# Regrouping the FFN chunks of a fp32 decoder: groups of three, a down projection by seven products in four parts, and a first group that adds into seeded banks

## Chip, cores and metric

The kernel runs on one core of a Trainium2 chip. The metric is device time in microseconds (us) of one execution. TensorE is called PE (its weight loads PEld), VectorE DVE, ScalarE ACT, GpSimd POOL, SyncE SP.

## The reference

A trunk of two layers over one sequence of 512 tokens with 1024 features (DEPTH 2, D_FF 2816), all in fp32. Each layer is an FFN at half weight, a mixer, and a second FFN at half weight; the mixer of layer 0 is a gated linear attention (GLA), that of layer 1 a stick-breaking attention (SB). A last RMSNorm follows.

```python
def swiglu(h, w_gate, w_up, w_down):
    return (jax.nn.silu(h @ w_gate) * (h @ w_up)) @ w_down
...
# Layer i: x += 0.5*FFN_a(RMSNorm(x)); x += Mixer(RMSNorm(x)); x += 0.5*FFN_b(RMSNorm(x))
```

The work thus runs FFN 1, GLA, FFN 2, FFN 3, SB, FFN 4, final norm.

## The kernel before

**fp32 from parts.** Each fp32 operand is cut into a high part (a cast to fp32r, by ScalarE: `wh` for weights, L534; `hh`, `nh`, `th` for activations, L1231) and the remainder (a subtraction on VectorE: `wl`, L535; `hl`, `nl`, `tl`, L1232). A product is three matmuls: high x high, low x high, high x low (`mm3`, L477). Weights are raw tiles (`raw` of 8x256 per partition, two buffers; `rawd` for the down projection, two buffers) loaded by SP (L500) and cut once, into pools of four wide tiles (`wh`, `wl`) or one small tile ("few").

**x** lies transposed in SBUF as eight tiles of 128 features x 512 tokens (`xs[0]` to `xs[7]`). PSUM has eight banks, handed out by tag (`ps_f`, `ps_d`, `ps_w`, `ps_z`, `ps_q` name the accumulators in the profile).

**An FFN** takes its 2816 features as 11 chunks of 256. For each chunk gate and up are formed, multiplied, cut (`close`, `close_first`, `close_second`), and later multiplied by the chunk's rows of `w_down`. Chunks are put into groups (L1042): while one group's gate and up are computed, the down products of the group before stand between them. Gate and up go in two ways: by direct products for the first two chunks, and by *seven products* for the other nine (`seven`, L1110): a 2x2 block product (features by halves of the tokens, 256 columns) of seven block products instead of eight, at the price of sums of weight blocks on VectorE (L1119 to L1126) and of copies between banks.

**The down projection** has the same two ways.

- *Direct* (`down`, L740 to L773): a bank `ps_d` of 128 x 512 sums over the group's features for one tile of x; when it is complete, VectorE adds half of it to x (L767).
- *Seven products* (`seven_down`, L775 to L872), for groups of two chunks that DOWN_SEVEN names. It runs in two parts of 256 columns of each half of `w_down`, so that one part serves x tiles m = 0, 1 of the part in both halves of the model (xs[k] and xs[k+4]). VectorE forms four sums of weight blocks (L796, L797, L803, L804). Then seven products of 2 chunks each (matmul L812) go, for each m, into three banks: w takes b11, is copied to z by ScalarE (L830), and then takes t2, t3 and t4, one after the other; after each of them VectorE adds the bank to a quarter of two x tiles (L818), and the next product adds onto the same bank. q takes t1 and b22, z takes b21. For t3 ScalarE copies the bank to `u3` first (L857). A product on a bank must wait until the bank's value before has been read.

In the last FFN the last group is written by tokens (`back_tok`).

**The order of the work.** Entries of a feed list say in which order weights are loaded and cut (`Entry.split`, L519; `Feed.ready`, L555 cuts for up to three entries ahead). Over this stands a `Planner`: it takes all recorded instructions, prices each (`price`, L171), plans each engine's order by these prices and due times, and pins that order. So a changed price moves instructions in every stage. At a stage's end the function `nxt` of the last group prepares the next one: ScalarE and VectorE form squares (L913, L914) and the cut of the scaled x (`xh` L924, `xl` L925) as each x tile is complete.

```python
        GROUPS = ((0, 2), (2, 4), (4, 6), (6, 7), (7, 9), (9, 11))
        DOWN_SEVEN = (1, 2, 4)
```

With these numbers six of 11 chunks (groups 1, 2 and 4) go down by seven products, the other five directly.

Of the kernel before, what the change touches and what calls it, by code (L numbers as in the profile page):

```python
# [48 lines left out]
class Planner:  # L49
# [31 lines left out]
    def gather(self):  # L81
# [11 lines left out]
        for i in self.bb.instructions:  # L93
# [7 lines left out]
            sizes, psum_in, wide = [], False, 0  # L101
            for write, refs in ((False, i.ins), (True, i.outs)):
                for r in refs:
# [3 lines left out]
                    ap = [(int(s), int(n)) for s, n in b.ap]  # L107
                    n = 1
# [50 lines left out]
            self.cost[k], self.step[k] = self.price(i, kind, e, sizes, psum_in)  # L159
# [11 lines left out]
    def price(self, i, kind, e, sizes, psum_in):  # L171
        n = max((s[1] for s in sizes), default=1)
        if e == "PE":
            types = [s[2] for s in sizes]
            if any("bfloat16" in t for t in types):
                return 270.0, max(64.0, 0.43 * n)
            if any("float32r" in t for t in types):
                return 165.0 + 0.42 * n, max(112.0, 0.422 * n)
            moving = sizes[0][1]
            full = sizes[1][1] == P and not kind.endswith("Transpose") and not getattr(i, "is_transpose", False)  # L180
            return 150.0 + 0.9 * n, max(58.0, 0.845 * moving) * (2 if full and moving in (1, P) else 1)
# [260 lines left out]
def decoder(ctx: ExitStack, tc: tile.TileContext, a: dict, out: bass.AP):  # L442
# [31 lines left out]
    def mm(ps, l, r, first, last):  # L474
        nc.tensor.matmul(ps, l, r, start=first, stop=last)  # L475

    def mm3(ps, wh, wl, mh, ml, first, last):  # L477
        mm(ps, wh, turns(mh), first, False)
        mm(ps, wl, turns(mh), False, False)
        mm(ps, wh, turns(ml), False, last)  # L480
# [5 lines left out]
    class Chunk:  # L486
# [51 lines left out]
    class Feed:  # L538
# [15 lines left out]
        def ready(self, i, gone):  # L554

            used = -gone
            for e in self.q[i : i + 3]:
                n = sum(n * m >= 1024 for _, _, n, m in e.units)
# [181 lines left out]
    def down(w, r0, nf, hs, part, nxt, late=0):  # L740
# [7 lines left out]
        def body(W):  # L748
# [3 lines left out]
            def prod(m, fs):  # L752
                if m == len(acc):
                    acc.append(psum("ps_d"))
                s = slice(m * P, (m + 1) * P)
                for f in fs:
                    mm3(acc[m], wh[:, f, s], wl[:, f, s], hs[f][0], hs[f][1], f == 0, f == nf - 1)
# [4 lines left out]
            for m in range(nd):  # L762
# [4 lines left out]
                nc.vector.scalar_tensor_tensor(  # L767
                    out=x, in0=flat(ps), scalar=0.5, in1=x, op0=ALU.mult, op1=ALU.add
                )
# [6 lines left out]
    def seven_down(pool, w, r0, hs, part):  # L776
# [16 lines left out]
        def sums_12(_):  # L793
            a11, _, a21, a22 = halves()
            s = v["s12"] = pool().tile([P, 4, 256], F32, tag="s", bufs=4, name="s12")
            nc.vector.tensor_tensor(out=s[:, 0:2], in0=a21, in1=a22, op=ALU.add)  # L796
            nc.vector.tensor_tensor(out=s[:, 2:4], in0=s[:, 0:2], in1=a11, op=ALU.subtract)  # L797
            return s

        def sums_34(_):  # L800
            a11, a12, a21, _ = halves()
            s = pool().tile([P, 4, 256], F32, tag="s", bufs=4, name="s34")
            nc.vector.tensor_tensor(out=s[:, 0:2], in0=a11, in1=a21, op=ALU.subtract)  # L803
            nc.vector.tensor_tensor(out=s[:, 2:4], in0=a12, in1=v["s12"][:, 2:4], op=ALU.subtract)  # L804
            return s

        def prod(ps, w, k0, m, b, first):
            for c in range(2):
                bh, bl = (turns(t) for t in hs[c][b])
                wh, wl = (t[:, k0 + c, m * P : (m + 1) * P] for t in w)  # L810
                for n, (l_, r_) in enumerate(((wh, bh), (wl, bh), (wh, bl))):
                    st["pe"] = nc.tensor.matmul(  # L812
                        ps, l_, r_, start=first and c + n == 0, stop=c == 1 and n == 2, skip_group_check=True
                    ).ins

        def add(m, up, col, ps):
            x = pair(xs[part * 2 + m + 4 * up][:, col * H : col * H + H])
            nc.vector.scalar_tensor_tensor(out=x, in0=ps, scalar=0.5, in1=x, op0=ALU.mult, op1=ALU.add)  # L818

        def body_1(W):  # L820
            a11, s, v["a2"] = W
            ws, zs, qs = [], [], []
            for m in range(2):
                ws.append(psum("ps_w")[:, 0:H])
                prod(ws[m], a11, 0, m, "b11", True)
            for m in range(2):
# [7 lines left out]
            for m in range(2):  # L834
                qs.append(ps[:, m * H : (m + 1) * H])
                prod(qs[m], s, 0, m, "t1", m == 0)
            for m in range(2):
                add(m, 1, 1, flat(qs[m]))
            yield
            for m in range(2):  # L840
                prod(ws[m], s, 2, m, "t2", False)
                add(m, 0, 1, flat(ws[m]))
            yield
            for m in range(2):
# [5 lines left out]
        def body_2(W):  # L850
            (s,) = W
            ws, qs = v["w"], v["q"]

            u3 = pool().tile([P, 2, H], F32, tag="c", bufs=1, name="u3")
            for m in range(2):
                prod(ws[m], s, 0, m, "t3", False)
                nc.scalar.copy(pair(u3[:, m]), flat(ws[m]))  # L857
                add(m, 1, 1, pair(u3[:, m]))
            yield
            for m in range(2):  # L860
                prod(qs[m], s, 2, m, "b22", False)
            for m in range(2):
                add(m, 0, 1, flat(qs[m]))
            yield
            for m in range(2):
                prod(ws[m], v["a2"], 2, m, "t4", False)
# [3 lines left out]
        units = [(lower, lambda t: halves()[0], 2, 256), (lower, sums_12, 4, 256), (lower, lambda t: halves()[1::2], 4, 256)]  # L870
        feed.q.append(Entry(units, body_1))
        feed.q.append(Entry([(lower, sums_34, 4, 256)], body_2))  # L872
# [162 lines left out]
    class FFN:  # L1035
# [6 lines left out]
        GROUPS = ((0, 2), (2, 4), (4, 6), (6, 7), (7, 9), (9, 11))  # L1042
        NORMED, SEVEN, AHEAD = 6, 2, 2
        DOWN_SEVEN = (1, 2, 4)
        SEVEN_UP = (2, 3, 4, 5, 6, 7, 8, 9, 10)

        def __init__(self, wg, wu, wd, gi, nxt, first=False, last=False):
            self.gi, self.normed = gi, False
            self.after_ffn = bool(phases) and isinstance(phases[-1], FFN)
            self.defer, self.gates = [], []  # L1050
# [4 lines left out]
            for group, (c0, c1) in enumerate(self.GROUPS):  # L1055
                slots, put = 2 * (c1 - c0), 0
                if group == 1:

                    for put in range(self.AHEAD):
                        down(*downs[put], late=put == 0)  # L1060
                    put = self.AHEAD
                for i in range(slots):
                    c, f = c0 + i // 2, i % 2
                    if f == 0:
# [17 lines left out]
                    if group - 1 in self.DOWN_SEVEN and f == 0 and c == c0:  # L1082
                        args = (lambda: self.tp, wd, self.GROUPS[group - 1][0] * 256, self.hs[group - 1])
                        seven_down(*args, 0)
                        seven_down(*args, 1)
# [5 lines left out]
                    while c >= self.SEVEN and put < len(downs) * (i + 1) // slots:  # L1091
# [6 lines left out]
                downs = [(wd, c0 * 256, n, self.hs[group], part, nxt if end else None) for part in range(n)]  # L1098
                if group in self.DOWN_SEVEN:
                    downs = []  # L1100
            self.count = len(feed.q) - base
# [182 lines left out]
        def close(self, t, group):  # L1284
            h = self.hp.tile([P, T], F32R, tag="hh", name="hh")
# [10 lines left out]
        def close_second(self, o0, o1, group):  # L1296
# [19 lines left out]
            if len(self.hs[group]) == 1:  # L1316
                for i in (2, 3):
                    h, l = (t[:, H:T] for t in self.n[i])
                    b[f"t{i + 1}"] = self.cut(h, l, ts[:, i])
            else:  # L1320

                h = sp.tile([P, T], F32R, tag="sq", name="t34")
                l = sp.tile([P, T], F32R, tag="ss", name="t34")
                self.cut(h, l, ts[:, 2:4].rearrange("p a b -> p (a b)"))
                b["t3"], b["t4"] = (h[:, 0:H], l[:, 0:H]), (h[:, H:T], l[:, H:T])

        def run(self, between=None):
            with tc.tile_pool(name="hp", bufs=8, reuse_waits="tile") as self.hp, tc.tile_pool(
                name="tp", bufs=5, reuse_waits="tile"
# [997 lines left out]
```

## Time and profile before

| | us |
|---|---|
| median of 3 runs (lowest, highest) | 1750.26 (1749.68, 1750.9) |
| the profiled execution, its own time | 1753.55 |
| its span, first to last instruction | 1751.6 |
| PE busy in the span | 1741.9 |
| DVE busy | 1586.3 |
| ACT busy | 1078.2 |
| FFN 1, 22.7 to 332.0: PE busy, DVE busy | 308.88, 300.73 |
| GLA, 343.0 to 547.0 | 203.99, 164.90 |
| FFN 2, 547.0 to 869.0 | 321.55, 308.79 |
| FFN 3, 869.0 to 1188.0 | 318.93, 304.42 |
| SB, 1188.0 to 1422.0 | 232.97, 179.67 |
| FFN 4, 1422.0 to 1720.0 | 298.00, 287.87 |

The span runs from the first to the last instruction; the rest of the execution's own time lies around it. "PE ps_q <- DVE x" in the list of waits is PE idle ahead of a matmul into ps_q that a VectorE write to x released. In a group's row, the figures behind the first bar are busy us and mean ns of one, behind the second the idle time of the engine just before them. In a timeline a row shows start, duration, engine, line, operation and the tiles (output <- inputs). A matmul's duration is longer than the step to the next, since they are pipelined. The window rows give, for each engine, busy us and instructions, then the granted clock of TensorE, the DMA engines' share and GB/s.

### The profile page before, as it was taken

How to read it: one execution, taken by the hardware profiler on the slowest of the kernel's cores; microseconds unless marked ns; L12 is line 12 of the kernel's file. 1: busy time of each engine (PE TensorE's matmuls, PEld its weight loads, DVE VectorE, ACT ScalarE, POOL GpSimd, SP SyncE). 2: the span in 40 equal slices, each digit the busy share in tenths (PEclk: the TensorE clock that was granted, in tenths of full speed). 3: DMA queues.
4: the chain of work that ended last, by engine and by line, in shares of the span. 5: the costliest groups of instructions: out<-in, count | busy, mean ns of one | idle time of the engine just before them, and what ended most of it. 6: DMA issues, size and time to landing. Idle time of an engine off the chain costs nothing.

```text
span 1751.6 us, 31640 instructions
## 1 busy us (share of the span) xinstructions
PE 1741.9 (99%) x12810; PEld 1630.5 (93%) x12810; DVE 1586.3 (91%) x2688; ACT 1078.2 (62%) x1898; POOL 9.9 (1%) x24
## 2 busy tenths in 40 slices
PE   9999999999999999999999999999999999999998
PEld 8999999888888999999989999999888889999997
DVE  8999999787888989999899999996898679999996
ACT  7556566554656565565655566566888755665655
POOL 0000000100000000000000000000000000000000
PEclk9999999999999999999999999999999999999999
DMA  6333333321223333333323333332222233333422
GB/s 190 125 98 120 97 122 121 106 70 53 73 97 97 121 116 102 97 121 113 126 77 119 99 107 121 109 103 79 61 73 73 73 97 121 121 97 104 130 93 73
DMA packets 176710, 179.27 MB, mean 102 GB/s; under 512 B 4082, under 2 KB 166180, under 8 KB 176564
## 3 DMA queue, kind: packets, MB, share of 16 engines
q1 hardware_dynamic: 175712, 175.91, 32.1%
q8 instruction: 100, 1.64, 0.4%
q0 software_dynamic: 608, 1.05, 0.2%
q14 instruction: 46, 0.38, 0.1%
q10 hardware_dynamic: 244, 0.29, 0.0%
HBM read 175.17 MB, written 2.10 MB: 101 GB/s over the span
## 4 chain that ended last, share of the span: by engine, by line
PE 85%; DVE 11%; ACT 1%; issue 1%; DMA 1%; DVEq 0%
PE ps_w L1134 18%; PE ps_f L475 17%; PE ps_d L475 10%; PE ps_q L1134 9%; PE ps_w L812 5%; PE ps_t L475 5%; PE ps_b L475 5%; PE ps_z L1134 5%; DVE wl L535 4%; PE ps_q L812 3%; DVE x L818 1%; PE ps_z L812 1%; PE ps_z L1815 1%; DMA rawd<-in_ffn_w_down_dram 1%; PE ps_S L475 1%
## 5 line engine op out<-in xcount | busy, mean ns | idle before, releaser
L535 DVE TENSOR_TENSOR wl<-raw,wh 128x1024 fp32r<-128x1024 f32 x241 | 256.5, 1066 | 42.0 <-ACT wh L534 41.4
L534 ACT CAST wh<-s 128x1024 fp32r<-128x1024 f32 x192 | 201.7, 1051 | 148.1 <-DVE s L1126 41.5
L534 ACT CAST wh<-raw 128x1024 fp32r<-128x1024 f32 x241 | 221.6, 921 | 78.6 <-PE ps_f L475 33.6
L1134 PE MATMUL ps_w<-th,wh 128*128 128x256 f32 x864 | 238.2, 276 | 0.2
L1134 PE MATMUL ps_w<-tl,wh 128*128 128x256 f32 x864 | 237.7, 275 | 0.0
L1134 PE MATMUL ps_w<-th,wl 128*128 128x256 f32 x864 | 237.7, 275 | 0.0
L535 DVE TENSOR_TENSOR wl<-s,wh 128x1024 fp32r<-128x1024 f32 x192 | 235.2, 1226 | 2.7 <-ACT wh L534 2.6
L475 PE MATMUL ps_f<-xh,wh 128*128 128x512 f32 x432 | 166.8, 386 | 0.0
L1134 PEld LDWEIGHTS ps_w<-th,wh 128*128 128x128 f32 x864 | 166.0, 192 | 0.7 <-ACT o L1167 0.7
L1134 PEld LDWEIGHTS ps_w<-tl,wh 128*128 128x128 f32 x864 | 166.0, 192 | 0.0
L1134 PEld LDWEIGHTS ps_w<-th,wl 128*128 128x128 f32 x864 | 166.0, 192 | 0.0
L475 PE MATMUL ps_f<-xl,wh 128*128 128x512 f32 x432 | 163.8, 379 | 0.0
L475 PE MATMUL ps_f<-xh,wl 128*128 128x512 f32 x432 | 163.8, 379 | 0.0
L475 PE MATMUL ps_d<-hh,wh 128*128 128x512 f32 x288 | 109.4, 380 | 0.0
L475 PE MATMUL ps_d<-hl,wh 128*128 128x512 f32 x288 | 109.3, 380 | 0.0
L475 PE MATMUL ps_d<-hh,wl 128*128 128x512 f32 x288 | 109.2, 379 | 0.0
L535 DVE TENSOR_TENSOR wl<-rawd,wh 128x512 fp32r<-128x512 f32 (+1 forms) x108 | 93.0, 867 | 1.4 <-ACT wh L534 1.4
L534 ACT CAST wh<-rawd 128x512 fp32r<-128x512 f32 (+1 forms) x108 | 80.6, 764 | 21.0 <-PE ps_d L475 12.0
L475 PEld LDWEIGHTS ps_f<-xl,wh 128*128 128x128 f32 x432 | 81.7, 189 | 11.5
L475 PEld LDWEIGHTS ps_f<-xh,wh 128*128 128x128 f32 x432 | 81.8, 189 | 11.0
L475 PEld LDWEIGHTS ps_f<-xh,wl 128*128 128x128 f32 x432 | 81.8, 189 | 10.7
L1134 PE MATMUL ps_q<-th,wh 128*128 128x256 f32 x288 | 79.3, 275 | 0.0
(349 smaller groups left out, 5506.1 us busy)
## 6 DMA issues: line engine op xcount, KB each, us to landing
raw<-in_ffn_w_gate_dram SPq DMA_DIRECT2D x43, 1024.0 KB, 5.4
raw<-in_ffn_w_up_dram SPq DMA_DIRECT2D x43, 1024.0 KB, 5.3
rawd<-in_ffn_w_down_dram SPq DMA_DIRECT2D x84, 512.0 KB, 3.5
raw<-in_gla_w_in_dram SPq DMA_DIRECT2D x12, 1024.0 KB, 5.2
raw<-in_sb_w_in_dram SPq DMA_DIRECT2D x16, 512.0 KB, 3.8
raw<-in_gla_w_out_dram SPq DMA_DIRECT2D x4, 1024.0 KB, 5.0
raw<-in_sb_w_in_dram SPq DMA_DIRECT2D x4, 1024.0 KB, 5.1
raw<-in_sb_w_out_dram SPq DMA_DIRECT2D x4, 1024.0 KB, 5.1
```

The source lines that it names most:

```text
L475: nc.tensor.matmul(ps, l, r, start=first, stop=last)
L534: nc.scalar.copy(h[:, k], part)
L535: nc.vector.tensor_tensor(out=l[:, k], in0=part, in1=h[:, k].bitcast(F32), op=ALU.subtract)
L812: st["pe"] = nc.tensor.matmul(ps, l_, r_, start=first and c + n == 0, stop=c == 1 and n == 2, skip_group_check=True).ins
L818: nc.vector.scalar_tensor_tensor(out=x, in0=ps, scalar=0.5, in1=x, op0=ALU.mult, op1=ALU.add)
L1134: st["pe"] = nc.tensor.matmul(o, l_, r_, start=first and j + n == 0, stop=j == 3 and n == 2, skip_group_check=True).ins
L1815: nc.tensor.matmul(o_, l_, r_, start=first, stop=last, skip_group_check=True)
```

## The change

1. **Groups.** Chunks are grouped 1, 3, 3, 3, 1 (last FFN: 1, 3, 3, 2, 2). Groups 1, 2 and 3 go down by seven products: nine chunks in FFN 1 to 3, eight in the last.
2. **Seven-product down in four parts.** With n chunks in a group a part takes 128 columns per half and one m (`per` = 1): each product is 3 chunks, 9 matmuls of 256 columns. The loads become 128x6x128 (384 KB). Sums and cuts become 384 and 768 columns. The last part of group 3 is held until just ahead of the last group's direct downs. Groups of two chunks keep `per` = 2.
3. **Seeded banks.** For the first group (one chunk), ScalarE writes 2x into the `ps_d` bank first (L761 of the changed kernel), the products accumulate onto it, and ScalarE writes the bank times 0.5 back to x (L777), in place of VectorE's add. In FFN 1 this holds for x tiles 2 to 7, in the others for all eight.
4. **Pools.** `rawd` has three buffers instead of two, the pool of temporaries four instead of five; a tile counts as small ("few") up to 512 columns, not below 1024. The cuts of t3 and t4 are joined, and lie in other tiles.
5. **Planner's prices.** Transposes, full fp32 matmuls and scans are priced differently.

The core of the diff:

```diff
-        GROUPS = ((0, 2), (2, 4), (4, 6), (6, 7), (7, 9), (9, 11))
+        GROUPS = ((0, 1), (1, 4), (4, 7), (7, 10), (10, 11))
+        LAST_GROUPS = ((0, 1), (1, 4), (4, 7), (7, 9), (9, 11))
+        SEEDED = (0,)
-        DOWN_SEVEN = (1, 2, 4)
+        DOWN_SEVEN = (1, 2, 3)
...
             def prod(m, fs):
                 if m == len(acc):
                     acc.append(psum("ps_d"))
+                    if part * nd + m >= seeds:
+                        x = pair(xs[part * nd + m])
+                        nc.scalar.activation(flat(acc[m]), x, AF.Copy, scale=2.0)
...
-                nc.vector.scalar_tensor_tensor(
-                    out=x, in0=flat(ps), scalar=0.5, in1=x, op0=ALU.mult, op1=ALU.add
-                )
+                if k >= seeds:
+                    nc.scalar.activation(x, flat(ps), AF.Copy, scale=0.5)
+                else:
+                    nc.vector.scalar_tensor_tensor(
+                        out=x, in0=flat(ps), scalar=0.5, in1=x, op0=ALU.mult, op1=ALU.add
+                    )
...
-    def seven_down(pool, w, r0, hs, part):
+    def seven_down(pool, w, r0, hs, part, n, per):
+        W_ = per * P
         lower, upper = (
-            Chunk(w[r0 : r0 + 4 * P, c : c + 256].rearrange("(f p) c -> p f c", p=P), 4, 256)
-            for c in (part * 256, 512 + part * 256)
+            Chunk(w[r0 : r0 + 2 * n * P, c : c + W_].rearrange("(f p) c -> p f c", p=P), 2 * n, W_)
+            for c in (part * W_, 512 + part * W_)
         )
...
-            for c in range(2):
+            for c in range(n):
...
-            for m in range(2):
+            for m in range(per):
                 ws.append(psum("ps_w")[:, 0:H])
...
+                        b0, b1 = self.GROUPS[group - 1]
+                        per = 2 if b1 - b0 == 2 else 1
+                        parts = [(*args, part, b1 - b0, per) for part in range(4 // per)]
+                        if group + 1 == len(self.GROUPS) and not last:
+                            held = parts.pop()
+                        for x in parts:
+                            seven_down(*x)
...
-                    self.t = st["few"].tile([P, self.n, self.m], F32, tag="rawd", bufs=2, name="rawd")
+                    self.t = st["few"].tile([P, self.n, self.m], F32, tag="rawd", bufs=3, name="rawd")
...
-                    few = n * m < 1024
+                    few = n * m <= 512
...
+            if i.is_transpose:
+                return 273.0, 109.0
+            if sizes[1][1] == P:
+                return max(362.0, 180.0 + 1.62 * moving), max(200.0, 1.7 * moving)
+            return 172.0 + 0.86 * moving, max(60.0, 0.85 * moving)
...
-            if "Scan" in kind:
+            if scan:
                 n *= 2
```

Where instructions move, by the order of the two programs. On VectorE, in the first seven-product part of the down projection of FFN 1 (s12 and s34 are the sums of weight blocks, wl the cuts' remainders, x4, x0 and so on the tiles of x) before:

```order
L796 TENSOR_TENSOR s12_1422<-rawd_1420 128x512
L535 TENSOR_TENSOR wl_1535<-rawd_1312,wh_1534 128x512
L818 SCALAR_TENSOR_TENSOR x4_85<-ps_q_1491,x4_85 128x256
L818 SCALAR_TENSOR_TENSOR x5_86<-ps_q_1491,x5_86 128x256
L818 SCALAR_TENSOR_TENSOR x0_81<-ps_w_1473,x0_81 128x256
L797 TENSOR_TENSOR s12_1422<-s12_1422,rawd_1312 128x512
L818 SCALAR_TENSOR_TENSOR x1_82<-ps_w_1480,x1_82 128x256
L803 TENSOR_TENSOR s34_1470<-rawd_1312,rawd_1420 128x512
L804 TENSOR_TENSOR s34_1470<-rawd_1312,s12_1422 128x512
L535 TENSOR_TENSOR wl_1539<-s12_1422,wh_1538 128x1024
```

And in the same place of the changed kernel:

```order
L831 SCALAR_TENSOR_TENSOR x4_85<-ps_q_1442,x4_85 128x256
L539 TENSOR_TENSOR wl_1474<-rawd_1235,wh_1473 128x384
L831 SCALAR_TENSOR_TENSOR x0_81<-ps_w_1430,x0_81 128x256
L809 TENSOR_TENSOR s12_1379<-rawd_1377 128x384
L816 TENSOR_TENSOR s34_1427<-rawd_1235,rawd_1377 128x384
L810 TENSOR_TENSOR s12_1379<-s12_1379,rawd_1235 128x384
L1214 TENSOR_TENSOR o0_1305<-ps_q_1303,o0_1305 128x256
L817 TENSOR_TENSOR s34_1427<-rawd_1235,s12_1379 128x384
L831 SCALAR_TENSOR_TENSOR x4_85<-u3_1507,x4_85 128x256
L831 SCALAR_TENSOR_TENSOR x0_81<-ps_z_1440,x0_81 128x256
L539 TENSOR_TENSOR wl_1478<-s12_1379,wh_1477 128x768
```

The adds now come one to a product instead of two, the pieces are 384 and 768 columns instead of 512 and 1024, and between two adds stand cuts and sums of the next part.

On VectorE, the first group's adds in FFN 1 before:

```order
L767 SCALAR_TENSOR_TENSOR x0_81<-ps_d_653,x0_81 128x512
L767 SCALAR_TENSOR_TENSOR x1_82<-ps_d_663,x1_82 128x512
L1125 TENSOR_TENSOR s34_726<-raw_601 128x512
L535 TENSOR_TENSOR wl_803<-s12_693,wh_802 128x1024
L1126 TENSOR_TENSOR s34_726<-raw_601,s12_693 128x512
L535 TENSOR_TENSOR wl_807<-raw_601,wh_806 128x1024
```

In the changed kernel ScalarE has this work for x tiles 2 to 7, the writes into the banks (L761) well ahead and the write-backs here:

```order
L777 ACTIVATE x2_83<-ps_d_672 128x512
L538 CAST wh_657<-raw_521 128x1024
L777 ACTIVATE x3_84<-ps_d_677 128x512
L777 ACTIVATE x4_85<-ps_d_715 128x512
L777 ACTIVATE x5_86<-ps_d_724 128x512
L777 ACTIVATE x6_87<-ps_d_733 128x512
L538 CAST wh_706<-s34_661 128x1024
```

Six VectorE additions per FFN 1 have become twelve ScalarE operations, which stand among its casts.

On SP, loads of gate, up and down weights in FFN 1 before:

```order
L500 DMA rawd<-in_ffn_w_down_dram 128x4x256 x4
L500 DMA raw<-in_ffn_w_up_dram 128x8x256
L500 DMA raw<-in_ffn_w_gate_dram 128x8x256
L500 DMA raw<-in_ffn_w_up_dram 128x8x256
L500 DMA raw<-in_ffn_w_gate_dram 128x8x256
L500 DMA rawd<-in_ffn_w_down_dram 128x4x256 x2
L500 DMA rawd<-in_ffn_w_down_dram 128x2x512 x2
```

And in the changed kernel:

```order
L504 DMA raw<-in_ffn_w_gate_dram 128x8x256
L504 DMA rawd<-in_ffn_w_down_dram 128x6x128 x8
L504 DMA raw<-in_ffn_w_up_dram 128x8x256
L504 DMA raw<-in_ffn_w_gate_dram 128x8x256
L504 DMA raw<-in_ffn_w_up_dram 128x8x256
L504 DMA raw<-in_ffn_w_gate_dram 128x8x256
L504 DMA raw<-in_ffn_w_up_dram 128x8x256
```

Eight loads of a group's down weights now stand in a row between a gate load and the up load behind it, where four did.

More of the change, by code (lines that the diff above doesn't have):

```diff
@@ L107, in gather @@
                     ap = [(int(s), int(n)) for s, n in b.ap]
+                    scan |= any(s < 0 for s, _ in ap)
                     n = 1
@@ L472, in decoder, with mm, mm3 @@
     xs = [xp.tile([P, T], F32, name=f"x{k}") for k in range(KD)]
[L474 to L480, printed above, removed]
+    def mm(ps, l, r, first, last, seeded=False):
+        nc.tensor.matmul(ps, l, r, start=first, stop=last, skip_group_check=seeded)
+    def mm3(ps, wh, wl, mh, ml, first, last, seeded=False):
+        mm(ps, wh, turns(mh), first, False, seeded)
+        mm(ps, wl, turns(mh), False, False, seeded)
+        mm(ps, wh, turns(ml), False, last, seeded)
     class Chunk:
@@ L557, in ready @@
             for e in self.q[i : i + 3]:
-                n = sum(n * m >= 1024 for _, _, n, m in e.units)
+                n = sum(n * m > 512 for _, _, n, m in e.units)
                 if used + n > 4:
@@ L738, in back, with down @@
                 feed.q.append(Entry([u], body))
-    def down(w, r0, nf, hs, part, nxt, late=0):
+    def down(w, r0, nf, hs, part, nxt, seeds, late=0):
         nd = KD // nf
@@ L754, in prod @@
                     acc.append(psum("ps_d"))
+                    if part * nd + m >= seeds:
+                        x = pair(xs[part * nd + m])
+                        nc.scalar.activation(flat(acc[m]), x, AF.Copy, scale=2.0)
                 s = slice(m * P, (m + 1) * P)
                 for f in fs:
-                    mm3(acc[m], wh[:, f, s], wl[:, f, s], hs[f][0], hs[f][1], f == 0, f == nf - 1)
+                    seeded = part * nd + m >= seeds
+                    first = f == 0 and not seeded
+                    mm3(acc[m], wh[:, f, s], wl[:, f, s], hs[f][0], hs[f][1], first, f == nf - 1, seeded)
             if late:
@@ L1048, in __init__ @@
             self.gi, self.normed = gi, False
+            if last:
+                self.GROUPS = self.LAST_GROUPS
             self.after_ffn = bool(phases) and isinstance(phases[-1], FFN)
-            self.defer, self.gates = [], []
+            self.defer, self.gates, self.first = [], [], None
             self.lead = []
@@ L1056, in __init__ @@
                 slots, put = 2 * (c1 - c0), 0
[L1057 to L1061, printed above, removed]
                 for i in range(slots):
                     c, f = c0 + i // 2, i % 2
+                    if (c, f) == (self.SEVEN, 0):
+                        for put in range(self.AHEAD):
+                            down(*downs[put], late=put == 0)
+                        put = self.AHEAD
                     if f == 0:
@@ L1097, in __init__ @@
                 end = group + 1 == len(self.GROUPS)
-                downs = [(wd, c0 * 256, n, self.hs[group], part, nxt if end else None) for part in range(n)]
+                seeds = KD if group not in self.SEEDED else 2 if first else 0
+                downs = [
+                    (wd, c0 * 256, n, self.hs[group], part, nxt if end else None, seeds)
+                    for part in range(n)
+                ]
                 if group in self.DOWN_SEVEN:
                     downs = []
+            if not last:
+                seven_down(*held)
             self.count = len(feed.q) - base
@@ L1284, in close @@
         def close(self, t, group):
+            if group in self.DOWN_SEVEN:
+                if self.first is None:
+                    self.first = t
+                else:
+                    self.close_first(self.first, group)
+                    self.close_second(self.first, t, group)
+                    self.first = None
+                return
             h = self.hp.tile([P, T], F32R, tag="hh", name="hh")
```

89 lines of the change are left out of this document (43 added, 46 removed).

## The prediction

> **What bounds the kernel now.** I read the page's head and the shares of the chain that ended last, then busy time by window of the four FFNs, then the chain, the waits and the DVE timeline inside them.
>
> ```profile
> span 1751.6 us, 31640 instructions
> PE 1741.9 (99%) x12810; PEld 1630.5 (93%) x12810; DVE 1586.3 (91%) x2688; ACT 1078.2 (62%) x1898; POOL 9.9 (1%) x24
> PE 85%; DVE 11%; ACT 1%; issue 1%; DMA 1%; DVEq 0%
> ```
>
> TensorE (PE) is busy 99% of the span and 85% of the chain; the 11% of DVE in the chain says that VectorE (DVE) feeds it with little to spare. By window (PE, PEld, DVE, ACT, POOL; the granted clock is 1.00 throughout):
>
> ```profile
> 22.70:332.00 309.30, 308.88 (x2402) 298.42 (x2403) 300.73 (x508) 186.59 (x326) 7.79 (x15) 1.00 0.35 110
> 547.00:869.00 322.00, 321.55 (x2457) 308.85 (x2456) 308.79 (x520) 194.54 (x336) 0.00 (x0) 1.00 0.35 111
> 869.00:1188.00 319.00, 318.93 (x2448) 307.11 (x2447) 304.42 (x513) 189.66 (x331) 0.53 (x1) 1.00 0.35 109
> 1422.00:1720.00 298.00, 298.00 (x2352) 288.44 (x2351) 287.87 (x490) 178.25 (x313) 0.53 (x1) 1.00 0.35 110
> sum 1248.30, PE 1247.36 PEld 1202.82 DVE 1201.81 ACT 749.04 POOL 8.86; mean PE 311.84 PEld 300.71 DVE 300.45 ACT 187.26 POOL 2.22
> 125.00:300.00 175.00, 174.58 (x1517) 173.14 (x1517) 174.06 (x309) 104.43 (x188) 0.00 (x0) 1.00 0.35 109
> ```
>
> In the FFNs PE idles 0.94 us in 1248.3. DVE idles 46.5 (8.57, 13.21, 14.58, 10.13). In 125 to 300 of the first FFN, the seven-product chunks, both run without a gap for 175 us: DVE can work with next to no idle time, and it is next to bind. So the change is a trade: matmuls away, DVE work added where DVE has 46.5 us and a lead.
>
> **The change, part by part.**
>
> *TensorE.* A direct chunk of down is 48 matmuls of 512 columns; by seven products it is 84 of 256. From the chain:
>
> ```profile
> 54.14 10.36 PE ps_d L475 x48
> 72.53 2.68 PE ps_w L1134 x24
> ```
>
> A 512-column step is 10.36/48 = 0.2158 us, a 256-column one 2.68/24 = 0.1117. So a chunk costs 48 x 0.2158 = 10.36 now and 84 x 0.1117 = 9.38 after: 0.98 less. Of 11 chunks six go by seven products before; nine after in FFN 1 to 3, eight in the last. Eleven chunks move: the two orders show 528 fewer ps_d matmuls and 924 more of 256 columns, 113.9 us out and 103.2 in, **-10.75** (-2.93, -2.93, -2.93, -1.96). [...]
>
> *VectorE.* Starts of neighbours in the DVE timeline:
>
> ```profile
> 186.12 0.70 DVE L803 TENSOR_TENSOR s<-rawd 128x512 f32<-128x512 f32 x1
> 186.72 0.70 DVE L804 TENSOR_TENSOR s<-rawd,s 128x512 f32<-128x512 f32 x1
> 187.32 1.23 DVE L535 TENSOR_TENSOR wl<-s,wh 128x1024 fp32r<-128x1024 f32 x1
> 188.46 0.76 DVE L818 SCALAR_TENSOR_TENSOR x<-ps_w,x 128x256 f32<-128x256 f32 x2
> ...
> 191.46 0.43 DVE L818 SCALAR_TENSOR_TENSOR x<-ps_q,x 128x256 f32<-128x256 f32 x1
> 191.79 0.43 DVE L818 SCALAR_TENSOR_TENSOR x<-ps_w,x 128x256 f32<-128x256 f32 x1
> ```
>
> An operation of 512 columns holds DVE for 0.60 us, of 1024 1.14, of 256 0.33; interpolated, 0.467 for 384 and 0.87 for 768. The two orders give the counts: adds of x from ps_d 88 to 26, -62 x 0.60 = -37.2 (ScalarE's seeds take 30 of these, the moved chunks the rest); cuts of hl, t and ts +23 x 0.60 = +13.8; sums and cuts of 512 -154 x 0.60 = -92.4; of 384 +308 x 0.467 = +143.8; of 768 +88 x 0.87 = +76.6; of 1024 -66 x 1.14 = -75.2; small ones +31 x 0.33 = +10.2. Sum **+39.6**, by FFN about +12.5, +11.3, +11.3, +4.4.
>
> With PE's time shrinking by 2.93, 2.93, 2.93 and 1.96, DVE must find 15.5, 14.2, 14.2 and 6.4 us. It has its idle time and the lead with which it stands ahead of PE at a stage's end. A weight cut there and its first use:
>
> ```profile
> 316.46 0.69 DVE L767 SCALAR_TENSOR_TENSOR x<-ps_d,x 128x512 f32<-128x512 f32 x1 [0.51 <-PE ps_d L475]
> 317.07 0.74 DVE L925 SCALAR_TENSOR_TENSOR xl<-x,gT,xh 128x512 fp32r<-128x512 f32 x1
> 317.73 1.22 DVE L535 TENSOR_TENSOR wl<-raw,wh 128x1024 fp32r<-128x1024 f32 x1
> ...
> 332.02 0.38 PE L475 MATMUL ps_f<-xh,wl 128*128 128x512 f32 x1
> ```
>
> From the cut's end to its use are 332.02 - 317.73 - 1.22 = 13.1 us. FFN 1: 8.57 idle + 13.1 lead - 15.5 leaves 6. FFN 2 and 3: 27.8 idle against 28.4: even, -0.6 (no lead counted). FFN 4: 10.1 against 6.4 leaves 3.7. So DVE still fits, if no more than about 9 us of idle time is forced upon it in the four. The stretch of 175 us with 0.94 idle says that this can be; I take no stall from it, bounds 0 and +26 (below).
>
> [...]
>
> *New tight loops.* Before, a part has two column blocks m, and between two products on one bank lie 2 m of another product. After, each part has one m and three chunks: a product is 9 matmuls, 9 x 0.1117 = 1.005 us, and the order on PE is strictly w, q, w, z, w, q, w. Between t2 and t3 on bank w lies one product of 1.0 us, in which DVE must add the bank to x (the last w matmul, its reader, the next PE step with its stall):
>
> ```profile
> 188.67 0.28 PE L812 MATMUL ps_w<-nl,wh 128*128 128x256 f32 x1
> 188.98 0.63 ACT L830 COPY ps_z<-ps_w 128x256 f32<-128x256 f32 x2
> ...
> 189.37 0.35 PE L812 MATMUL ps_q<-hh,wh 128*128 128x256 f32 x1 [0.42 <-DVE x L818]
> ```
>
> ```profile
> PE ps_q L812 <- DVE x L818: 0.8, 2, 0.4
> ```
>
> ```profile
> L830 ACT COPY ps_z<-ps_w 128x256 f32<-128x256 f32 x48 | 17.0, 358 | 14.2 <-PE ps_w L812 13.8
> ```
>
> A reader starts 0.31 after the last issue, 0.20 after its step, and takes 0.43: 0.63 of 1.005, so 0.37 is left. DVE's queue is in order, and a 768 cut of 0.87 us ahead of the add breaks it. A missed turn costs 189.37 - 188.67 - 0.11 = 0.59 us. Today PE waits twice for these adds (us in all, count, mean), in 48 column blocks (the count of the z copies), with twice the room. I take three times that rate, 6 of 46 parts: 6 x 0.59 = **+3.5**; bounds 0 and 28 of 46, +16.5.
>
> *DMA.* DVE's rawd wait and two loads:
>
> ```profile
> DVE s L796 <- DMA rawd<-in_ffn_w_down_dram: 5.9, 7, 2.1
> ```
>
> ```profile
> rawd<-in_ffn_w_down_dram SPq DMA_DIRECT2D x84, 512.0 KB, 3.5
> raw<-in_sb_w_in_dram SPq DMA_DIRECT2D x16, 512.0 KB, 3.8
> ```
>
> The parts now load 384 KB in rows of 512 B. The nearest rows are 3.5 us (512 KB) and 3.8, so about 3.5 us; a part takes 63 x 0.1117 = 7.04 us and uses two loads, with three buffers instead of two. DMA is 35% busy. On SP eight of these loads now stand in a row before the next up load, so a late buffer delays that load too, but it is a whole chunk (28 us) ahead. Cost 0, bounds 0 and +4 (seven such waits of 0.6 each).
>
> *ScalarE.* Per operation:
>
> ```profile
> L534 ACT CAST wh<-s 128x1024 fp32r<-128x1024 f32 x192 | 201.7, 1051 | 148.1 <-DVE s L1126 41.5 <-DVE s L1120 36.6 <-DVE s L797 27.8
> L534 ACT CAST wh<-rawd 128x512 fp32r<-128x512 f32 x72 | 42.9, 623 | 0.0
> ```
>
> Interpolated, 384 columns take 0.52 and 768 0.84. Casts: -66 x 1.05 - 66 x 0.62 + 132 x 0.52 + 88 x 0.84 = +32; 30 seeds and 30 write-backs x 0.62 = +37; cuts of hh +9. ACT goes from 749 to about 827 of 1238: 67%. Cost 0: its idle time of some 490 us hides it. The write-backs lie beside the second chunk group's first matmuls; a late one holds a bank only.
>
> *The last group of one chunk.* Each of eight banks is now 6 matmuls, 1.295 us, while DVE does x add 0.60, then xl and ss for each:
>
> ```profile
> L925 DVE SCALAR_TENSOR_TENSOR xl<-x,gT,xh 128x512 fp32r<-128x512 f32 x40 | 29.5, 748 | 1.4 <-ACT xh L924 1.4
> L914 DVE SCALAR_TENSOR_TENSOR ss<-ss,sq 128x512 f32<-128x512 f32 x35 | 24.0, 687 | 0.5 <-ACT sq L913 0.2
> ```
>
> That is 0.60 + 0.66 + 0.60 = 1.87 by starts (x add to xl 0.61, xl to its successor 0.66, in the rows at 316.46 and 317.07), so DVE falls 8 x 0.57 = 4.6 us behind PE in the end of a stage. Cost 0, since the 13.1 us of lead covers it, and up to 3 x 4.6 = +14 if the lead is gone.
>
> *Outside the FFNs* the planner's prices for transposes and full fp32 matmuls and its test for scans change the order:
>
> ```profile
> 1188.00:1422.00 234.00, 232.97 (x1443) 198.19 (x1442) 179.67 (x264) 178.85 (x346) 0.00 (x0) 1.00 0.24 73
> ```
>
> PE idles 1.0 us of 234 here, so there is little to win: 0, bounds -1.5 and +1.5.
>
> **Sum.** -10.75 + 3.5 = -7.25. The profiled execution's span of 1751.6 goes to 1744.3; its own time, 1753.55, lies 1.95 above its span and becomes 1746.3. It is 3.29 above the median of the three runs, 1750.26, which becomes **1743.0**.
>
> **Rivals.** (The bound for a change is 0.2%, 3.5 us, about what a measurement of this kernel can tell from no change.)
>
> *Full gain*, no turn missed: -10.75, with up to -1.5 from the new order: 1738 to 1739.5. For it, DVE's 175 us without a gap; against, margins of 0.37 us beside cuts of 0.87. With the range's lower part, 0.2.
>
> *Used up*: 16 missed turns, 16 x 0.59 = 9.4, or 10 us of forced DVE idle above the 9: 1748.9 to 1749.5. Chance 0.16.
>
> *DVE binds*, the slower side: adds, casts and PE run in a ring with DVE in the middle, and its idle time stays, since it comes from waits for ACT's cast, the buffer and PE's bank. Above 9 us every further us of idle moves PE's end; at 9 + 10.75 = 20 of today's 46.5 the gain is gone. If three quarters stay (35), PE stalls 26 and the time is 1750.26 - 10.75 + 26 = 1765.5. For it: after +39.6 DVE needs 1241.4 us of windows of 1237.5, more than there is, and lives on the lead. Against: most of the idle lies at the start and the end of FFNs, while the middle of the first had 0.94. Chance 0.08.
>
> *Every DVE operation holds the engine for its whole duration* (0.43 where 0.33 lie between starts: 0.10 more). Then the addition is 39.6 + 168 x 0.10 = 56.4, 17 more, which passes the spare 9 by 8, and the time is 1743.0 + 8 = 1751.0. But the 508 operations of the first window would need 300.73 + 50.8 = 351.5 us of 309.30: no chance. [...]
>
> *Missed turns decide*: 10.75 / 0.59 = 18 of 46 undo the gain; 28 give +16.5 - 10.75 = +5.7, 1756.0. Chance 0.05.
>
> That the change does not do what it says is excluded by the matmul counts of the order.
>
> **How the numbers follow.** Forecast's own case 0.51, full gain 0.2, used up 0.16, slower 0.13. The range goes from 1738 to 1752: it takes in full gain and used up, and leaves out most of the slower cases and a little of the new order's gain, some 0.2. Faster by over 0.2%: 0.71; within: 0.16; slower: 0.13.
>
> **What would show it.** Right: about 528 fewer ps_d matmuls; PE's FFN windows shorter by 2 to 3 us each; DVE's idle time there below 10 us; some six waits of PE w or q for DVE's x add, of 0.4 to 0.6. Wrong: PE idle of over 8 us in the FFN windows, on wl (DVE binds) or on x adds and the ACT copies (turns); DVE waiting for rawd above 10 us; a gap of PE where one FFN ends and the next begins.

## The result and the profile after

The changed kernel takes 1741.45 us (median of 4 runs, 1738.83 to 1741.9) against 1750.08 for the kernel before (1749.68 to 1750.9): the ratio is 0.9945 [0.9933, 0.9956], 8.6 us less. The prediction said 1743.0. The profiled execution took 1741.74, with a span of 1740.0. The profiled execution of before was 3.5 us above this median, so the two profiles lie 11.6 us apart by span, and differences between them are read by stage.

The head of the page and the shares of the chain, changed kernel:

```profile
span 1740.0 us, 32878 instructions
...
PE 1729.9 (99%) x13206; PEld 1633.0 (94%) x13206; DVE 1618.7 (93%) x2856; ACT 1142.1 (66%) x2056; POOL 10.0 (1%) x24
...
PE 91%; DVE 7%; ACT 1%; DMA 1%; issue 1%; DVEq 0%; ACTq 0%; SPq 0%
```

PE's busy time fell by 12.0 us, DVE's rose by 32.4, ACT's by 63.9. The chain is PE for 91% of its length instead of 85%. The four FFNs by window (columns as before):

```profile
22.73:329.18 306.45, 306.44 (x2508) 299.39 (x2509) 305.31 (x546) 196.74 (x358) 7.88 (x15) 1.00 0.35 108
544.86:861.42 316.56, 316.47 (x2559) 308.48 (x2558) 312.21 (x556) 209.51 (x375) 0.00 (x0) 1.00 0.37 115
861.42:1178.14 316.72, 316.71 (x2559) 308.10 (x2558) 314.95 (x560) 205.38 (x371) 0.54 (x1) 1.00 0.36 108
1409.95:1708.20 298.25, 297.51 (x2428) 289.77 (x2427) 291.77 (x516) 193.60 (x348) 0.54 (x1) 1.00 0.36 111
sum 1237.98, PE 1237.13 PEld 1205.74 DVE 1224.24 ACT 805.23 POOL 8.96; mean PE 309.28 PEld 301.43 DVE 306.06 ACT 201.31 POOL 2.24
```

DVE's idle time in the FFNs went from 46.5 to 13.7 us. It does 22.4 us more inside these windows; the other 10 us lie outside them, 6.3 in the GLA and 3.8 in the stick-breaking stage, since DVE now ends a stage later. That shows in the last cut of x at the end of FFN 1 and its first use on PE. Before:

```profile
334.29 0.75 DVE L925 SCALAR_TENSOR_TENSOR xl<-x,gT,xh 128x512 fp32r<-128x512 f32 x1
...
339.36 0.38 PE L475 MATMUL ps_f<-xl,wh 128*128 128x512 f32 x1
```

And after (the second of the two cuts in this row ends at 335.80):

```profile
334.39 1.41 DVE L941 SCALAR_TENSOR_TENSOR xl<-x,gT,xh 128x512 fp32r<-128x512 f32 x2
...
336.74 0.38 PE L479 MATMUL ps_f<-xl,wh 128*128 128x512 f32 x1
```

The lead went from 4.3 to 0.9 us. Where the time went by stage, from the first matmul of each stage in the traces (us), beside the kernel before with the new planner prices alone (the third experiment below):

| | before | before, new prices | after |
|---|---|---|---|
| start to the first down product | 53.97 | 52.15 | 53.84 |
| rest of FFN 1 | 277.83 | 277.84 | 275.34 |
| GLA | 215.26 | 215.29 | 215.68 |
| FFN 2 | 320.86 | 319.08 | 316.56 |
| FFN 3 | 319.73 | 319.20 | 316.72 |
| SB | 233.86 | 231.81 | 231.81 |
| FFN 4 and end | 330.07 | 329.86 | 330.00 |
| span | 1751.6 | 1745.2 | 1740.0 |

At equal prices the rest of the change is worth 2.5 us in each of the first three FFNs and nothing in the fourth. The stick-breaking stage gained 2.05 from the prices. The start varies by up to 2 us between executions (51.97 to 53.97 over those profiled), and that is no effect of the change.

The DVE timeline in a part of the new down projection shows the new pieces; 207.84 to 208.31 is 0.47 us for 384 columns, 209.92 to 210.78 is 0.86 for 768:

```profile
207.84 0.55 DVE L816 TENSOR_TENSOR s<-rawd 128x384 f32<-128x384 f32 x1
208.31 0.55 DVE L810 TENSOR_TENSOR s<-s,rawd 128x384 f32<-128x384 f32 x1
...
209.92 0.94 DVE L539 TENSOR_TENSOR wl<-s,wh 128x768 fp32r<-128x768 f32 x1
210.78 0.55 DVE L539 TENSOR_TENSOR wl<-rawd,wh 128x384 fp32r<-128x384 f32 x1
```

And the waits in the parts (us in all, count, longest), with the loads:

```profile
DVE s L809 <- DMA rawd<-in_ffn_w_down_dram: 1.7, 7, 0.4
...
PEld ps_q L825 <- DVE wl L539: 0.5, 2, 0.3
...
PEld ps_w L825 <- DVE x L831: 0.2, 1, 0.2
```

```profile
rawd<-in_ffn_w_down_dram SPq DMA_DIRECT2D x88, 384.0 KB, 3.5
```

PE is held by an add to x just once, for 0.2 us. DVE's wait for rawd fell from 5.9 to 1.7 us.

### The profile page after: what moved, and what is told of

The parts are those of the page before. It is cut to its first block, busy times and chain, and to the rows that moved or that the text cites. A ratio compares the mean times of both kernels' runs of the same rounds, so it can differ in the third digit from the quotient of the medians.

```text
span 1740.0 us, 32878 instructions
## 1 busy us (share of the span) xinstructions
PE 1729.9 (99%) x13206; PEld 1633.0 (94%) x13206; DVE 1618.7 (93%) x2856; ACT 1142.1 (66%) x2056; POOL 10.0 (1%) x24
## 4 chain that ended last, share of the span: by engine, by line
PE 91%; DVE 7%; ACT 1%; DMA 1%; issue 1%; DVEq 0%; ACTq 0%; SPq 0%
PE ps_w L1164 21%; PE ps_f L479 15%; PE ps_q L1164 10%; PE ps_w L825 10%; PE ps_q L825 5%; PE ps_z L1164 5%; PE ps_t L479 5%; PE ps_b L479 4%; PE ps_d L479 4%; PE ps_z L825 3%; DVE wl L539 2%; PE ps_z L1849 2%; PE ps_oT L1934 1%; PE ps_T L1919 1%; PE ps_bt L479 1%; PE ps_S L479 1%
## 5 line engine op out<-in xcount | busy, mean ns | idle before, releaser
L538 ACT CAST wh<-s 128x1024 fp32r<-128x1024 f32 (+1 forms) x236 | 229.2, 971 | 113.4 <-PE ps_q L1164 28.1
L539 DVE TENSOR_TENSOR wl<-s,wh 128x1024 fp32r<-128x1024 f32 (+1 forms) x236 | 263.1, 1115 | 1.6 <-ACT wh L538 1.4
L539 DVE TENSOR_TENSOR wl<-rawd,wh 128x384 fp32r<-128x384 f32 (+2 forms) x152 | 92.6, 614 | 1.1 <-ACT wh L538 1.1
L825 PE MATMUL ps_w<-hh,wh 128*128 128x256 f32 x324 | 90.5, 279 | 0.0
L825 PE MATMUL ps_w<-hh,wl 128*128 128x256 f32 x324 | 89.1, 275 | 0.0
L825 PE MATMUL ps_w<-hl,wh 128*128 128x256 f32 x324 | 89.1, 275 | 0.0
L538 ACT CAST wh<-rawd 128x384 fp32r<-128x384 f32 (+2 forms) x152 | 84.6, 566 | 4.1 <-PE ps_f L479 1.8
L1164 PE MATMUL ps_w<-nh,wl 128*128 128x256 f32 x288 | 79.2, 275 | 0.0
```

The costliest lines, as they stand in the source:

```text
L538: nc.scalar.copy(h[:, k], part)
L539: nc.vector.tensor_tensor(out=l[:, k], in0=part, in1=h[:, k].bitcast(F32), op=ALU.subtract)
L825: nc.tensor.matmul(ps, l_, r_, start=first and c + i == 0, stop=c == n - 1 and i == 2, skip_group_check=True)
L1164: st["pe"] = nc.tensor.matmul(o, l_, r_, start=first and j + n == 0, stop=j == 3 and n == 2, skip_group_check=True).ins
```

## The experiments

Two theories stood against each other from the start. *Balance*: the gain is TensorE's matmul arithmetic, and it can be had only as far as VectorE is kept at TensorE's pace; the seeds pay for the regrouping. *Order and room*: VectorE still has room, and what moved the time is the planner's new order. In every run below the planner orders the program anew, so what a run shows is the effect of its work and of its order together.

**No seeds.**

```diff
-        SEEDED = (0,)
+        SEEDED = ()
```

> The changed kernel without the seeded banks: 30 adds of 0.60 us come back to VectorE (18.0 us), 60 operations leave ScalarE; TensorE's matmuls are the same. Theory (VectorE stands at its limit beside TensorE: 13.7 us idle in the four FFN windows, leads of 0.1 us in the down parts): 1746 to 1753 us, with TensorE waiting for VectorE. Rival (VectorE still has room): as the changed kernel, 1741.5 within 1.5.

Measured: 1757.83 us, ratio to before 1.0043 [1.003, 1.0055]. That is 16.4 us above the changed kernel, for 18.0 us of added VectorE work, and more than the range expected. Its FFN windows in sum, and what PE waited for in the parts:

```profile
sum 1253.60, PE 1244.76 PEld 1207.62 DVE 1240.26 ACT 778.17 POOL 8.95; mean PE 311.19 PEld 301.90 DVE 310.06 ACT 194.54 POOL 2.24
```

```profile
PE ps_w L825 <- ACT u L869: 6.0, 9, 0.9
...
PE ps_q L825 <- DVE wl L539: 0.9, 4, 0.3
```

DVE idles 13.3 us, hardly less than with the seeds. So the 13.7 us that are left are not room: DVE gives next to none of them up. PE idles 8.8 us instead of 0.85, and what releases it in name is most often ScalarE's copy of the t3 product to `u`. ScalarE has less to do in this kernel, so the cause is not its load. The copy itself waits for VectorE, here first without the seeds, then in the changed kernel:

```profile
ACT u L869 <- DVE o L1210: 30.9, 10, 3.4
```

```profile
ACT u L869 <- DVE o L1210: 2.8, 1, 2.8
```

There is one buffer for `u`, which gate and up (L1209) share with the down projection (L869), so a copy must wait until VectorE has added the value before it. Ahead of all nine of PE's waits the copy had stood still for such an add, eight times for L1210 and once for L831. PE thus waits for VectorE, by way of ScalarE. A second buffer for `u` was not run. Without the seeds the regrouping is slower than the kernel before.

**The old prices in the changed kernel, and the new prices in the kernel before.** In the first, `price` is that of before; in the second, that of the change.

> The changed kernel with the planner's prices of before. Theory (the gain is TensorE's matmul arithmetic in the FFNs): 1741.5 within 1.5. Rival (the new prices give the 2.0 us by which the stick-breaking stage became shorter): 1743.5, with that stage back at 233.9.

> The kernel before with the new planner prices alone. Theory: 1750 within 1.5. Rival (prices give 2.0 us of the gain): 1748, with the stick-breaking stage at 231.8 instead of 233.9.

Measured: 1743.39 (ratio 0.9958 [0.9946, 0.9971]) and 1747.55 (0.9985 [0.9977, 0.9994]). In both pairs the kernel with the new prices has the stick-breaking stage at 231.81 and the one with the old prices at 233.86. The row of that stage before, then with the new prices alone:

```profile
1187.70:1421.50 233.80, 232.77 (x1441) 198.03 (x1440) 179.47 (x265) 178.49 (x345) 0.00 (x0) 1.00 0.24 72
```

```profile
1183.70:1415.50 231.80, 231.80 (x1442) 197.84 (x1441) 177.38 (x265) 179.51 (x346) 0.00 (x0) 1.00 0.24 73
```

The rival is right here: 2 us of the gain are the planner's (1.9 and 2.65 by the medians). In that stage PE has 1.0 us less of visible idle time, and as much again was won within what counts as busy.

**VectorE's work in the parts raised.** The first weight sum of each part is made twice.

```diff
             nc.vector.tensor_tensor(out=s[:, 0:n], in0=a21, in1=a22, op=ALU.add)
+            nc.vector.tensor_tensor(out=s[:, 0:n], in0=a21, in1=a22, op=ALU.add)
```

> The changed kernel with the first weight sum of each down part made twice: 44 x 0.467 + 2 x 0.60 = 21.7 us more for VectorE inside the parts, the same result. Theory (VectorE at its limit): 13.7 us of idle at most can take it, so 8 to 18 us slower, 1750 to 1760. Rival (VectorE has room): 1741.5 within 1.5.

Measured: 1766.06 (1.0088 [1.0073, 1.0103]), 24.6 us above the changed kernel for 21.7 us of added work, above the range expected. No time is absorbed. PE now waits in the parts for adds and cuts, among others:

```profile
PE ps_q L826 <- DVE x L832: 2.9, 7, 0.4
...
PE ps_q L826 <- DVE wl L539: 2.3, 8, 0.6
```

**VectorE's work in the parts lowered.** The first sum is a ScalarE copy of one summand; the second summand is left out.

```diff
-            nc.vector.tensor_tensor(out=s[:, 0:n], in0=a21, in1=a22, op=ALU.add)
+            nc.scalar.copy(s[:, 0:n], a21)
```

> The changed kernel with the first weight sum of each down part replaced by a ScalarE copy of one summand, so that the second summand is left out: VectorE does 21.7 us less, ScalarE 24 us more, TensorE the same. Theory (TensorE and VectorE stand in balance: time goes one to one up with added VectorE work, but down only by the stalls that TensorE has left in the FFNs, 4.9 us): 1736.5 to 1741. Rival (VectorE alone sets the time): 1720 to 1725.

Measured: 1741.39 (0.995 [0.9937, 0.9964]), as the changed kernel. The windows in sum:

```profile
sum 1237.27, PE 1234.46 PEld 1202.47 DVE 1207.36 ACT 827.80 POOL 8.95; mean PE 308.62 PEld 300.62 DVE 301.84 ACT 206.95 POOL 2.24
```

DVE is 17 us less busy in the same windows and idles 30 us; nothing is gained. But the run brings waits of its own, of which the changed kernel has next to none:

```profile
ACT s L809 <- DMA rawd<-in_ffn_w_down_dram: 14.0, 17, 2.4
...
PE ps_w L825 <- DVE x L831: 2.0, 3, 1.1
```

The copy stands in ScalarE's queue and waits there for loads, and PE waits for adds to x. So this run alone does not show that relief is worth nothing. What bounds it is PE's own work: in the changed kernel the steps of PE from one matmul to the next in the four FFNs add up to 4.5 us more than 0.1117 us for each of 256 columns and 0.2159 for each of 512, so at these steps no relief of VectorE could bring more there. That decides against VectorE alone setting the time. Up the time goes about one to one, down by 4.5 us at most: the changed kernel stands on the corner between two engines.

**The sum on GpSimd**, which is busy for 10.0 of the 1740.0 us of the changed kernel, with nothing left out.

```diff
-            nc.vector.tensor_tensor(out=s[:, 0:n], in0=a21, in1=a22, op=ALU.add)
+            nc.gpsimd.tensor_tensor(out=s[:, 0:n], in0=a21, in1=a22, op=ALU.add)
```

> The changed kernel with the first weight sum of each down part on GpSimd, which is idle: VectorE 21.7 us less, nothing left out. Theory (balance): 1736.5 to 1741 if a GpSimd sum takes up to some 2 us and disturbs nobody. Rival (GpSimd is slow, or VectorE runs slower while it works): 1742 to 1765.

Measured: 1776.03 (1.0145 [1.0132, 1.0159]), 34.6 us above the changed kernel. Groups of this run, then its waits:

```profile
L809 POOL TENSOR_TENSOR s<-rawd 128x384 f32<-128x384 f32 x44 | 81.4, 1850 | 1429.8 <-DVE wl L539 1104.1 <-DMA rawd<-in_ffn_w_down_dram 265.8 <-ACT o L1174 47.2
...
L816 DVE TENSOR_TENSOR s<-rawd 128x384 f32<-128x384 f32 x44 | 27.8, 631 | 14.6 <-DMA rawd<-in_ffn_w_down_dram 14.5
```

```profile
PE ps_w L825 <- DVE x L831: 23.3, 26, 3.0
...
DVE s L810 <- POOL s L809: 15.3, 24, 0.9
```

A sum takes 1.85 us on GpSimd and 0.55 on VectorE. VectorE has its next sum (L810) behind it, waits for GpSimd 24 times, and in its queue stand the adds to x. PE then waits for these adds 26 times, 23.3 us. VectorE also waits 14.5 us for loads ahead of L816, and not at all there in the changed kernel. This is the missed turn of the prediction, and it comes when VectorE's queue stands still, not from the short loop by itself.

**Two buffers of rawd.**

```diff
-... tag="rawd", bufs=3, name="rawd")
+... tag="rawd", bufs=2, name="rawd")
```

> The changed kernel with two rawd buffers instead of three. Theory (a part's loads then start only when the sums of the part before are made, 3.5 us of load in a part of 7.04 us, and VectorE has no time to wait): VectorE waits 0.5 to 1 us for rawd in each of 46 parts, TensorE is delayed, 1750 to 1790. Rival (loads are hidden with two as before): 1741.5 within 1.5.

Measured: 1768.62 (1.0101 [1.0087, 1.0115]), 27 us above the changed kernel. ScalarE and DVE wait for the loads, and PE for cuts:

```profile
ACT wh L538 <- DMA rawd<-in_ffn_w_down_dram: 19.4, 16, 2.3
...
DVE s L809 <- DMA rawd<-in_ffn_w_down_dram: 7.5, 15, 1.7
...
PE ps_w L825 <- DVE wl L539: 4.6, 4, 1.7
```

The third buffer is needed. DVE's wait for rawd grew by only 5.8 us, but that of ScalarE's casts grew from 0.5 to 19.4, and VectorE's cuts, which PE waits for, stand behind these casts. How much of the 27 us this makes, and how much the new order, is left open.

**The groups of before.** The changed kernel with the old groups, with seeds and then without:

```diff
-        GROUPS = ((0, 1), (1, 4), (4, 7), (7, 10), (10, 11))
-        LAST_GROUPS = ((0, 1), (1, 4), (4, 7), (7, 9), (9, 11))
+        GROUPS = ((0, 2), (2, 4), (4, 6), (6, 7), (7, 9), (9, 11))
+        LAST_GROUPS = ((0, 2), (2, 4), (4, 6), (6, 7), (7, 9), (9, 11))
...
-        DOWN_SEVEN = (1, 2, 3)
+        DOWN_SEVEN = (1, 2, 4)
```

> The changed kernel with the chunk groups of before (six chunks by seven products, parts of two column blocks), seeds, pools and prices kept: TensorE does the matmuls of before, VectorE 18 us less. Theory (the gain is TensorE's 10.75 us, seeds only make room for it): 1747 to 1750. Rival (seeds and order are the gain): 1741 to 1743.

> The changed kernel with the chunk groups of before and no seeds; its prices, pools and joined cuts stay. Theory (of the changes only the prices and the regrouping move the time): 1747.5 within 1.5, as the kernel before with the new prices. Rival (pools and cuts cost or gain something): outside that.

Measured: 1748.07 (0.9988 [0.9979, 0.9997]) and 1747.87 (0.9987 [0.9978, 0.9996]). In the kernel with seeds x is not fully carried through 12 of its 30 seeded banks (see the last section); only its time is used here. With the two runs of the new groups this is a square, all with the new prices and pools:

| us | no seeds | seeds |
|---|---|---|
| groups of before | 1747.87 | 1748.07 |
| groups of three | 1757.83 | 1741.45 |

The seeds alone bring nothing, the groups alone cost 10.0, both together bring 6.4. Pools and joined cuts move nothing by themselves (1747.87 against 1747.55 for the new prices alone).

**Seeds for the last group too**, and the same with one matmul of 512 columns with the start flag into each of these banks ahead of the seed:

```diff
-        SEEDED = (0,)
+        SEEDED = (0, 4)
...
+                        if nxt is not None:
+                            mm(acc[m], wh[:, 0, m * P : (m + 1) * P], turns(hs[0][0]), True, True)
```

(The second hunk is in the second kernel only.)

> The changed kernel with the last group of FFN 1 to 3 seeded too: 22 more adds (13.2 us) from VectorE to ScalarE, at the stage ends where the lead of the cut of x is 0.1 to 0.9 us. Theory (VectorE at its limit, its leads gone at the ends): 1738.5 to 1741. Rival (the ends hang on ScalarE, which makes squares and casts there): 1742 to 1746.

> As the kernel with the last group seeded too, with one matmul of all 512 columns with the start flag into each of the last group's 22 banks ahead of the seed (its value is overwritten by the seed). In the kernel without it these banks had last been started by products of 256 columns, and x was not fully carried through them. Theory on the seeds: with a start over the whole bank the seed is kept, as in the first group, whose banks were all last started with 512 columns; rival: the seed is lost for another reason. Theory on time: 22 x 0.216 = 4.75 us on TensorE, 1745 to 1747; rival (VectorE's relief of 13.2 us pays for it): 1741.

Measured: 1740.9 (0.9946 [0.9934, 0.9959]) and 1744.78 (0.9968 [0.9957, 0.9979]). In the first, x is not fully carried through the last group's 22 banks (see the last section); in the second it is. So taking 13.2 us from VectorE at the stage ends brings 0.5 us, not more than the runs scatter, and the 22 matmuls cost 3.9 of their 4.75. Neither is a better kernel.

**One more chunk by seven products in the last FFN.**

```diff
-        LAST_GROUPS = ((0, 1), (1, 4), (4, 7), (7, 9), (9, 11))
+        LAST_GROUPS = ((0, 1), (1, 4), (4, 7), (7, 10), (10, 11))
```

> The changed kernel with groups 1, 3, 3, 3, 1 in the last FFN too: one more chunk by seven products (TensorE 0.98 us less), some 7 us more of VectorE work there. By TensorE alone 1740.5; with VectorE at its limit (6.5 us idle in that window now) 1741 to 1746.

Measured: 1741.79 (0.9951 [0.9938, 0.9963]), no difference. The last FFN and the end take 329.93 us, 330.00 in the changed kernel. No version that was run beats the changed kernel by more than the scatter of the runs.

## Why the prediction was right, and where not

**TensorE, -10.75: right in its rates.** The steps of the 2940 half products are 0.112 us as predicted; the matmuls of 512 columns into `ps_d` fell by 528. The three FFNs that were to give 2.93 each gave 2.5 each against the kernel with equal prices; the fourth was to give 1.96 and gave nothing. Of the 10.75, 6.4 us arrived by the medians with equal prices.

**VectorE, +39.6: right in its durations, wrong in the room.** 384 columns take 0.47, 768 take 0.87. Busy time rose by 32.4 only. The sum counted from start to start, while an operation ahead of an idle gap is busy for its whole duration, 0.08 us more (0.55 against 0.47); VectorE has 314 gaps instead of 396, and 82 x 0.08 = 6.6 is most of the difference. The step that failed is the sentence that DVE still fits if no more than about 9 us of idle time is forced upon it. 13.7 us were left, and the runs without seeds and with the doubled sum show that next to none of them can be used: 18.0 us more cost 16.4, 21.7 cost 24.6. By my own working, 13.7 - 9 = 4.7 us should then be lost, and 4.4 are missing; that the 4.4 come about in that way is not shown. The lead was taken too large as well: the 13.1 us lie between a cut of weights and its use, but the last cut of x in FFN 1 was only 4.3 us ahead of its use. I counted idle time as spare, when it was made of waits that stay.

**The missed turns, +3.5: a give-back of about that size, by another way.** Against equal prices 4.4 us of the 10.75 are missing, but PE's wait for an add to x is a single one of 0.2 us. What the traces show instead, against the kernel before with the new prices: in each of FFN 1 to 3 some six to eleven of PE's steps come late, which makes about 0.4 us more a stage, and in FFN 4 PE waits for the cut of the normed input:

```profile
1445.93 0.38 PE L479 MATMUL ps_f<-nl,wh 128*128 128x512 f32 x1
1446.61 0.48 PE L479 MATMUL ps_f<-nh,wh 128*128 128x512 f32 x1 [0.30 <-ACT nh L1261]
...
1447.70 0.48 PE L479 MATMUL ps_f<-nl,wh 128*128 128x512 f32 x1 [0.39 <-DVE nl L1262]
```

These are 0.5 us twice (1446.61 - 1445.93 - 0.22 = 0.46, and 0.77 - 0.22 = 0.55 ahead of 1447.70). The rest of FFN 4's 2 us is not attributed. In the order as planned, the margin of 0.37 us in the new loop was enough.

**Outside the FFNs, 0 with bounds of 1.5: mis-sized.** The new prices brought 2.65 us [1.1, 4.0], of which 2.05 lie in the stick-breaking stage. I took PE's visible idle time there, 1.0 us, for all there was to win, but a slower step inside a busy stretch is no idle time.

**DMA, ScalarE and the last group, 0 each: right.** The loads take 3.5 us as estimated, with three buffers; with two they would have cost 27. ScalarE is busy 65% of the FFN windows. The end of FFN 1 used up the lead of the last cut of x down to 0.9 us, without a stall.

So 1743.0 came out 1.6 us from the measured time, and that it is so near is in part luck: the gain from the prices that I had put at 0 more than made up a give-back 0.9 us larger than mine. *DVE binds* was the rival nearest to the truth: it is what happens without the seeds, and with them the kernel stands at its edge.

## What to carry to other kernels

When a change takes work from the busiest engine and gives work to the second, a third engine must take over what the second has no room for, or the second becomes the first: here 18 us moved to ScalarE turned 10.0 us slower into 6.4 us faster. The idle time of an engine that feeds a saturated one is not spare until an experiment that adds work has shown it, and one run each way (work added, work removed) says on which side of the corner a kernel stands, if the run that removes work adds no waits of its own. Changes that come together are separated by a square of runs, not by the sum of single ones.

## What the runs showed of the hardware

In these kernels a bank that ScalarE had filled was added onto in full where the last matmul with the start flag on that bank had covered all its 512 columns, and not where it had covered 256. By the order on PE, all 30 seeded banks of the changed kernel had last been started with 512 columns. In the kernel with the last group seeded, 22 banks had last been started by a half product of 256, and the result came out with a relative error of 1.016; in the kernel with the groups of before and seeds this holds for 12 of 30, and the relative error was 0.627. One matmul of 512 columns with the start flag ahead of the seed in the 22 banks mended it, though its value is overwritten; but for the planner's order nothing else differs between the two kernels, so it was in these banks that x got lost. Why the width of the last start decides, no run shows.

A sum of two 384-column tiles took 1.85 us on GpSimd, 3.4 times VectorE's 0.55. VectorE's sum L816 of the same size took 0.63 us on average in that run and 0.55 in the changed kernel. It ran beside a GpSimd sum in 26 of its 44 cases; there it took 0.69 us on average and up to 1.37, in the other 18 it took 0.55. VectorE's adds to x (L831), which read PSUM, took 0.42 beside a GpSimd sum and without one.
